# A hybrid encoder block on one core: the memory values computed as a pair of chunks by block products

## The chip, the cores and the metric

The kernel runs on one core of one Trainium2 chip. The metric is the device time of one execution in microseconds (us); lower is better. A core has a matrix engine (TensorE, PE in the profile, with its weight loads as PEld), VectorE (DVE), ScalarE (ACT), GpSimd (POOL) and SyncE (SP), and sixteen DMA engines that SP's, ACT's and POOL's queues feed.

## The reference, cut to what matters

One residual block on x of 256 tokens by 1024 channels, float32: a feed-forward network (SwiGLU, 2816 wide), a mixer (a gated linear recurrence, HGRN2, beside a forgetting attention, FoX, merged by two gates), a cross attention that reads a memory of 256 rows, and a second feed-forward network. Each branch is normalised before and after by a root mean square. The part that is changed most:

```python
def mem_cross_attention(h, mem_n, w_mq, w_mkv, w_mo):
    q = (h @ w_mq).reshape(B, S, MEM_HEADS, MEM_DH)
    k, v = jnp.split(mem_n @ w_mkv, 2, axis=-1)
    ...
    s = jnp.einsum('bqhd,bkhd->bhqk', q, k) * (1.0 / math.sqrt(MEM_DH))
    p = jax.nn.softmax(s, axis=-1)
    o = jnp.einsum('bhqk,bkhd->bqhd', p, v).reshape(B, S, D_MODEL)
    return o @ w_mo

x = x + rmsnorm(mem_cross_attention(rmsnorm(x, mem_pre_g), rmsnorm(mem, mem_kv_g), ...), mem_post_g)
```

## The kernel before, in words

**Numbers as pairs.** Every float32 operand is split into a rounded high part and the rest (`hi` and `lo`, for activations `h` and `l` of a `Pair`), and each product is three matmuls: high by high, high by low, low by high. A weight unit is 128 x 1024 values, 512 KB. `load_split` loads one to a `raw` buffer (four of them), on SP's queue (line 136); ScalarE casts it to `hi` (137) and VectorE makes `lo` by subtraction (138); there are eight buffers each of `hi` and `lo`. `split` does the same for activations (156 and 157). All matmuls are issued on line 93 and recorded in `log`, so the profile has one line for nearly all of them.

**Order.** Each engine runs its own list of instructions in order. The program order is that of the code, but `after(i)` puts what follows it right behind the recorded matmul number i, ahead of what was written before it, and `issue_after` ties one instruction behind another; the constants at the head of the file (`L_...`, `F_T`, `M_O`, `SUMS_AT`) are these places. SP's queue holds the weight loads in order of use, each issued when its buffer comes free.

**Block products.** In pairs of chunks of the feed-forward networks (`quad`), an input of two halves is multiplied with two chunks of weights by seven products of blocks instead of eight: `forms_of`-like sums of the input's blocks are made once (in `mixed`), sums of the weights' blocks are either made on the spot or, for the second network, ahead of time. Three accumulators take part: `b1`, `b2` of the tag `mm` (two buffers) and `b3` of the tag `tr`. `b1` collects the first product, then the second on top of it, then the third, then the fourth; between these, `keep` copies its contents with ScalarE to a `z2` tile.

**Sums made ahead.** A step (`load_step`, `at`) loads two weight units into a `wide` buffer (two of them), adds their blocks by four additions of 128 x 512 on VectorE (lines 771 to 774) and stores them to device memory (776). There are 16 steps, four for each of the four pairs `QUADS_2` of the second feed-forward network, placed by `SUMS_AT` after named projections. The first two steps' loads go on SP's queue, the others' and all stores on POOL's (759, 776). `sum_of` loads the sums back into a `wide` buffer when the pair is computed (450), on SP's queue.

**Stages, in order.** First network; projections `i_a`, `f_a`, `q_a`; the recurrence's chunks interleaved with the projection `gf`; `k_b`, `q_b`, `v_b` of FoX; the four `gates` chunks, with FoX's outputs between them; `br_a` and `br_b`; `w_out`; then the memory block: keys `mk`, queries `mq`, values `mv`, scores, output `mo`; then the second network. The memory, transposed, comes in as `memT` and is multiplied by the gain into the pair `M`; its reciprocal root mean squares `rm` come from a second copy, `ms`. `mk` multiplies each product by the row `rowm` of these and then splits it; `mem_v(c)` (two chunks, 48 matmuls of 128 x 512 each) scales by `rm` when it leaves the accumulator (lines 1236 and 1237). The scores of the two token halves (maxima 1254, exponentials 1258, division 1260, transposes 1264) stand between `mem_v(0)` and `mem_v(1)`; the four `mem_out(i)` multiply probabilities with values, two of them placed inside `mem_v(1)`.

**The end.** `post_last` normalises the last half: sums of squares on ScalarE (243), a square root (357, table of its own), a reciprocal and one Newton step on VectorE (364 to 368), and the last addition into `xs` in three parts, one by ScalarE and POOL with its store on ACT's queue, two on VectorE with stores on SP's. `warm` calls a square root earlier (417), behind the Silu of the last chunk's second half as the code orders it, to load its table.

Of the kernel before, what the change touches and what calls it, by code (L numbers as in the profile page):

```python
# [42 lines left out]
M_O = (24, 36)  # L43
# [16 lines left out]
TO_GATES = 4  # L60
# [18 lines left out]
def block_kernel(ctx: ExitStack, tc: tile.TileContext, wts, head_in, gf_in, x_in, mem_in, memT_in, cols, rows, fbias, masks, out):  # L79
# [44 lines left out]
    loads = []  # L124

# [3 lines left out]
    def load_split(src, n=512):  # L129

        raw = wp.tile([P, D], F32, tag="raw", name=nm("raw"), bufs=4)
        hi, lo = parts_of()
        r, h, l = raw, hi, lo
        if n < 512:
            r, h, l = (p.rearrange("p (k n) -> p k n", k=2)[:, :, :n] for p in (raw, hi, lo))
        loads.append(nc.sync.dma_start(r, src).ins)
        S.copy(h, r)  # L137
        V.tensor_tensor(out=l, in0=r, in1=h.bitcast(F32), op=ALU.subtract)  # L138
        return hi, lo
# [134 lines left out]
    def mixed(X, r, back=0):  # L274

        with after(len(log) - 1 - back):
            row = row_of(r)
        full = [m4([P, 4, T], n="full") for _ in range(2)]
        for f, xh, xl in zip(full, X.h, X.l):
            V.tensor_tensor(out=f, in0=xh.bitcast(F32), in1=xl.bitcast(F32), op=ALU.add)  # L280
            V.tensor_tensor(out=f, in0=f, in1=bc(row, [P, 4, T], 1), op=ALU.mult)
        N = Pair()
        for q in range(2):
            split(N.h[q], N.l[q], full[q])
# [22 lines left out]
        return N, out  # L307
# [38 lines left out]
    def post_last(ps, h, grow, factor):  # L346
# [22 lines left out]
        for eng, a, b, queue in ((G, 512, 768, nc.scalar), (V, 0, 512, nc.sync), (V, 768, 1024, nc.sync)):  # L369
            xh = xs[:, h, a:b]  # L370
            t = ts[a // 512][:, a % 512 : a % 512 + b - a]
            if eng is G:
                S.activation(t, t, AF.Copy, scale=r)
                G.tensor_tensor(out=xh, in0=t, in1=xh, op=ALU.add)
            else:
                V.scalar_tensor_tensor(out=xh, in0=t, scalar=r, in1=xh, op0=ALU.mult, op1=ALU.add)  # L376
            queue.dma_start(out[h * P : (h + 1) * P, a:b], xh)


    def ffn(w_in, w_dn, X, r2, n_tok, i_row, quads, sums, first_half, second_half=None):  # L380
# [28 lines left out]
        def act_evac(ps, c, h):  # L409
# [5 lines left out]
            if c == NFF - 1 and (c, 1 - h) in ats and not first_half:  # L415
# [11 lines left out]
        def quad(c, n_down):  # L427
# [5 lines left out]
            def two(src):  # L433
                hi, lo = (p.rearrange("p (i n) -> p i n", i=2) for p in parts_of())
                split(hi, lo, src)
                return [(hi[:, i], lo[:, i]) for i in range(2)]

            B11, B21 = [], []

            if sums:  # L440
                for i in range(4):
                    hi, lo = load_split(wts[_AT[w_in] + 4 * c + i - 4])
                    B11.append((hi[:, :512], lo[:, :512]))
                    B21.append((hi[:, 512:], lo[:, 512:]))

                def sum_of(k):
                    W = wp.tile([P, 2, D], F32, tag="wide", name=nm("wide"), bufs=2)
                    for q in range(2):
                        with tc.issue_after(loads[-1]):
                            loads.append(nc.sync.dma_start(W[:, q], sums[c][(0, 3, 2, 1)[k], q]).ins)  # L450
                    return two(W[:, 0].rearrange("p (i n) -> p i n", i=2)) + two(W[:, 1].rearrange("p (i n) -> p i n", i=2))

                def lower():
                    out = []
                    for q in range(2):
                        u = _AT[w_in] + 4 * c + 2 * q
                        raw = wp.tile([P, D], F32, tag="raw", name=nm("raw"), bufs=4).rearrange("p (i n) -> p i n", i=2)
                        loads.append(nc.sync.dma_start(raw, wts[u : u + 2, :, 512:].rearrange("i p n -> p i n")).ins)
                        out += two(raw)
                    return out  # L460

                summed = None
            else:
                wide, made = [], [[], [], []]
# [38 lines left out]
            def X(h, j):  # L503
                hs = slice(h * P, h * P + P)
                return lambda i: (N.hi(2 * i + j)[:, hs], N.lo(2 * i + j)[:, hs])

            def F(h, l):
                return lambda i: (h[:, i], l[:, i])

            def prod(ps, A, B, i, start, stop=False):  # L510
                (ah, al), (bh, bl) = A(i), B[i]
                MM(ps, ah, bh, start=start and i == 0, stop=False, skip_group_check=True)
                MM(ps, ah, bl, start=False, stop=False, skip_group_check=True)
                MM(ps, al, bh, start=False, stop=i == 3, skip_group_check=True)

            def prods(ps, A, B, start, stop=False):
                for i in range(4):
                    prod(ps, A, B, i, start, stop)

            def keep(ps):  # L520
                t = sp.tile([P, 512], F32, tag="z2", name=nm("keep"), bufs=3)
                S.copy(t, ps)
                return t

# [609 lines left out]
    for j in range(2):  # L1134
        nc.sync.dma_start(memT_s[j], memT_in[:, 4 * j : 4 * j + 4, :])
# [261 lines left out]
```

## Time and profile before

| | us |
|---|---|
| three runs | 785.2, 785.71, 786.02 |
| the profiled execution | 785.17 |
| its span | 783.4 |
| TensorE busy | 774.3 (99%) |
| VectorE busy | 646.2 (82%) |
| ScalarE busy | 468.4 (60%) |
| GpSimd busy | 48.4 (6%) |
| DMA: mean rate, bytes | 247 GB/s, 193.61 MB |

Busy figures are shares of the span. In rows of groups, the columns are: line, engine, operation, output and inputs with shapes, count, then busy time in all, mean duration of one in ns, and the idle time of the engine just before them with what ended most of it. A timeline row has start, duration, engine, line, operation and count; a chain row has start, length and what ran. In the slices of the span (40 of 19.6 us each) a digit is a busy share in tenths. A row of DMA issues ends with the median time from issue to landing. In the table of windows, each engine's busy time stands in the order PE, PEld, DVE, ACT, POOL, then the granted clock, the DMA share and GB/s.

### The profile page before, as it was taken

The page shows a single profiled execution, that of the slowest core. Times are in us where ns is not written, and L with a number is a line of the kernel's source. Part 1 is how long each engine was busy: PE and PEld are TensorE (multiplying, and loading weights), DVE is VectorE, ACT ScalarE, POOL GpSimd, SP SyncE. Part 2 cuts the span into 40 slices and gives each one's busy share as a digit, 9 for nine tenths or more (in the row PEclk, how much of TensorE's full clock was granted, in tenths as well). Part 3 has the DMA queues.
Part 4 walks back from the last instruction along what each step waited for, and adds up shares of the span by engine and source line. Part 5 has one row for each costly group of instructions (what it writes and reads, how often), then busy time and mean ns, then how long its engine had stood idle before and what let it go on. Part 6 is the DMA issues. An engine that isn't in the chain of part 4 may idle for free.

```text
span 783.4 us, 13175 instructions
## 1 busy us (share of the span) xinstructions
PE 774.3 (99%) x5004; PEld 669.9 (86%) x5004; DVE 646.2 (82%) x1004; ACT 468.4 (60%) x704; POOL 48.4 (6%) x81
## 2 busy tenths in 40 slices
PE   9999999999999999999999999999999999999996
PEld 7888888888899999998888888999888888888884
DVE  7889989968798898578777886998787889888864
ACT  7665664756752447347674444744646758677763
POOL 0000000000121100200001221011110000000000
PEclk9999999999999999999999999999999999999999
DMA  9794484476687655753479999579875279899831
GB/s 349 249 327 154 155 309 161 147 233 245 251 305 257 183 191 164 232 212 121 152 278 341 377 338 378 203 275 375 319 226 185 83 261 388 311 314 323 339 122 54
DMA packets 57392, 193.61 MB, mean 247 GB/s; under 512 B 6249, under 2 KB 9713, under 8 KB 57329
## 3 DMA queue, kind: packets, MB, share of 16 engines
q1 hardware_dynamic: 48080, 159.60, 57.9%
q0 software_dynamic: 9104, 33.04, 12.1%
q8 instruction: 39, 0.64, 0.3%
q14 instruction: 25, 0.20, 0.1%
q10 hardware_dynamic: 144, 0.13, 0.0%
HBM read 174.92 MB, written 17.83 MB: 246 GB/s over the span
## 4 chain that ended last, share of the span: by engine, by line
PE 99%; ACT 0%; DVE 0%; issue 0%; DVEq 0%; ACTq 0%
PE mm L93 64%; PE acc L93 28%; PE tr L93 4%; PE tr L395 1%; PE tr L315 1%; PE tr L1067 0%; PE tr L1158 0%; PE tr L1264 0%; ACT L357 0%; PE tr L406 0%; DVEq L1393 0%; DVE xs L376 0%; ACT hT L156 0%; ACT y L357 0%; ACT junk L243 0%
## 5 line engine op out<-in xcount | busy, mean ns | idle before, releaser
L138 DVE TENSOR_TENSOR lo<-raw,hi 128x1024 fp32r<-128x1024 f32 (+1 forms) x228 | 271.3, 1205 | 53.0 <-ACT hi L137 49.2
L137 ACT CAST hi<-raw 128x1024 fp32r<-128x1024 f32 (+1 forms) x228 | 232.1, 1036 | 118.2 <-PE mm L93 69.5
L93 PE MATMUL mm<-lo,hT 128*128 128x512 f32 (+1 forms) x448 | 171.2, 386 | 0.0
L93 PE MATMUL mm<-hi,hT 128*128 128x512 f32 (+1 forms) x448 | 170.7, 385 | 0.0
L93 PE MATMUL mm<-hi,lT 128*128 128x512 f32 (+1 forms) x448 | 170.4, 384 | 0.0
L93 PE MATMUL acc<-hi,act 128*128 128x512 f32 x352 | 113.2, 391 | 0.0
L93 PE MATMUL mm<-hT,hi 128*128 128x256 f32 x384 | 109.0, 284 | 0.1
L93 PE MATMUL mm<-hT,lo 128*128 128x256 f32 x384 | 109.0, 284 | 0.0
L93 PE MATMUL mm<-lT,hi 128*128 128x256 f32 x384 | 108.9, 284 | 0.0
L93 PEld LDWEIGHTS mm<-hi,hT 128*128 128x128 f32 x448 | 84.1, 188 | 16.1 <-ACT hT L271 0.7
L93 PEld LDWEIGHTS mm<-hi,lT 128*128 128x128 f32 x448 | 84.1, 188 | 15.8 <-DVE lT L272 0.5
L93 PEld LDWEIGHTS mm<-lo,hT 128*128 128x128 f32 x448 | 84.0, 188 | 15.0 <-DVE lo L138 0.4
L93 PEld LDWEIGHTS acc<-hi,act 128*128 128x128 f32 x352 | 65.9, 188 | 13.7 <-DVE act L157 0.2
L93 PEld LDWEIGHTS mm<-hT,hi 128*128 128x128 f32 x384 | 73.6, 192 | 0.5 <-issue 0.3
L93 PEld LDWEIGHTS mm<-lT,hi 128*128 128x128 f32 x384 | 73.6, 192 | 0.1
L93 PEld LDWEIGHTS mm<-hT,lo 128*128 128x128 f32 x384 | 73.6, 192 | 0.1
L93 PE MATMUL acc<-lo,act 128*128 128x512 f32 x176 | 69.0, 392 | 0.0
L157 DVE TENSOR_TENSOR lo<-wide,hi 128x1024 fp32r<-128x1024 f32 x40 | 47.9, 1219 | 1.5 <-ACT hi L156 1.1
L156 ACT CAST hi<-wide 128x1024 fp32r<-128x1024 f32 x40 | 41.5, 1052 | 11.5 <-DVE wide L494 7.5
L776 POOL DMA_DIRECT2D sums<-wide x32 | 23.6, 738 | 357.8 <-DVE wide L773 240.8
L93 PEld LDWEIGHTS acc<-lo,act 128*128 128x128 f32 x176 | 33.1, 188 | 6.7
L93 PE MATMUL mm<-hi,sh 128*128 128x512 f32 x96 | 37.5, 390 | 0.0
(243 smaller groups left out, 1126.8 us busy)
## 6 DMA issues: line engine op xcount, KB each, us to landing
raw<-in_wts_dram SPq DMA_DIRECT2D x232, 512.0 KB, 5.1
sums<-wide POOLq DMA_DIRECT2D x32, 512.0 KB, 6.2
wide<-sums SPq DMA_DIRECT2D x32, 512.0 KB, 6.9
wide<-in_wts_dram POOLq DMA_DIRECT2D x28, 512.0 KB, 6.7
wide<-in_wts_dram SPq DMA_DIRECT2D x12, 512.0 KB, 6.4
raw<-in_gf_dram SPq DMA_DIRECT2D x12, 344.0 KB, 4.9
head<-in_head_dram SPq DMA_DIRECT2D x8, 388.0 KB, 5.7
grow<-in_rows_dram SPq DMA_DIRECT2D x4, 512.0 KB, 8.9
```

The source lines that it names most:

```text
L93: log.append(PE.matmul(*args, **kw).ins)
L137: S.copy(h, r)
L138: V.tensor_tensor(out=l, in0=r, in1=h.bitcast(F32), op=ALU.subtract)
L156: S.copy(hi, src)
L157: V.tensor_tensor(out=lo, in0=src, in1=hi.bitcast(F32), op=ALU.subtract)
L315: PE.transpose(ps[:, j * P : (j + 1) * P], src(kb), ident)
L395: PE.transpose(trv[:, j, h * P : (h + 1) * P], ats[c, h][:, j * P : (j + 1) * P], ident)
L776: G.dma_start(sums[u][2 * e : 2 * e + 2, q, :, i * 512 : i * 512 + 512].rearrange("k p n -> p k n"), W[:, e])
```

## The change

1. The memory values become one pair of chunks in block form. `M` is scaled by `rowm` before it is split (`scale_by`), so `mk` and the values need no scaling of their own; `joined(M)` and `forms_of` make the four sums of `M`'s blocks; `summed_ahead("mv")` loads four weight units, the sums and the lower halves; the scores stand between the products. The helpers of `quad` move out of it unchanged.
2. Four steps of sums more, for this pair, ahead of the others: 20 steps at other places (`SUMS_AT`), the first after `i_a` and six of them among `q_a`, `gf` and FoX's projections, where there were none. A step's loads and stores now all go on SP's queue: the store six weight loads after the additions are written, the next load four later (`later`, `tick`).
3. `brow`, `memT` and `ms` are loaded from POOL's queue instead of SP's; `brow` uses a `z2` tile.
4. Work moves from VectorE to ScalarE: the affine maps of `f` and `k`, `q` by one Silu, `gf` by one Silu, FoX's division by the row sum.
5. `post_last` adds on VectorE alone, in two halves of 512, with both stores on SP's queue; `warm` stands behind the last Silu that is issued.
6. All four `mem_out` stand behind the products; the transposes of probabilities are placed inside them (`L_PT`).

The core of the diff:

```diff
-SUMS_AT = (
-    ("i_a", 1), ("f_a", 0), ("f_a", 2), ("f_a", 3), ("gates", 1), ("gates", 3), ("br_a", 0), ("br_b", 0),
-    ("br_a", 1), ("br_b", 1), ("mk", 1), ("mk", 3), ("mq", 0), ("mq", 1), ("mv", 1), ("ao", 0),
-)
+SUMS_AT = (("i_a", 1), ("f_a", 1), ("f_a", 3), ("q_a",1), ("q_a",3), ("gf",1), ("gf",3), ("gf",5), ("k_b", 1), ("q_b", 1), ("v_b", 3), ("gates", 0), ("gates", 1), ("gates", 2),("gates",3), ("br_a", 0), ("br_b", 0), ("br_a", 1), ("br_b", 1), ("mk", 3),)
+TO_STORE = 6
+TO_LOAD = 4
...
+    def later(n, f):
+        due.append((len(loads) + n, f))
+
+    def tick():
+        while due and due[0][0] <= len(loads):
+            due.pop(0)[1]()
...
+    def joined(X):
+        full = [m4([P, 4, T], n="full") for _ in range(2)]
+        for f, xh, xl in zip(full, X.h, X.l):
+            V.tensor_tensor(out=f, in0=xh.bitcast(F32), in1=xl.bitcast(F32), op=ALU.add)
+        return full
...
+    def scale_by(full, row):
+        for f in full:
+            V.tensor_tensor(out=f, in0=f, in1=bc(row, [P, 4, T], 1), op=ALU.mult)
...
-        for eng, a, b, queue in ((G, 512, 768, nc.scalar), (V, 0, 512, nc.sync), (V, 768, 1024, nc.sync)):
...
+        for j, (t, xh) in enumerate(zip(ts, x_halves(h))):
+            V.scalar_tensor_tensor(out=xh, in0=t, scalar=r, in1=xh, op0=ALU.mult, op1=ALU.add)
+            nc.sync.dma_start(out[h * P : (h + 1) * P, j * 512 : (j + 1) * 512], xh)
...
-            if c == NFF - 1 and (c, 1 - h) in ats and not first_half:
+            if len(ats) == 2 * NFF - 1 and not first_half:
                 with tc.issue_after(silu.ins):
                     S.activation(warm, ones[:, 0:1], AF.Sqrt)
...
+    pairs = [("mv", 0)] + [("f2_in", c) for c in QUADS_2]
...
-                if len(slots) < 2:
-                    with tc.issue_after(loads[-1]):
-                        nc.sync.dma_start(part, src)
-                else:
-                    G.dma_start(part, src)
+            with tc.issue_after(loads[-1]):
+                nc.sync.dma_start(W[:, e].rearrange("p j n -> p (j n)"), wts[_AT[name] + 4 * (c + e - 1) + 2 * q + i])
...
-        for e in range(2):
-            G.dma_start(sums[u][2 * e : 2 * e + 2, q, :, i * 512 : i * 512 + 512].rearrange("k p n -> p k n"), W[:, e])
-        load_step()
+        def store():
+            for e in range(2):
+                with tc.issue_after(loads[-1]):
+                    nc.sync.dma_start(sums[u][2 * e : 2 * e + 2, q, :, i * 512 : i * 512 + 512].rearrange("k p n -> p k n"), W[:, e])
+            later(TO_LOAD, load_step)
+        later(TO_STORE, store)
...
-                V.tensor_scalar(out=f[:, i], in0=f[:, i], scalar1=olb[:, hd : hd + 1], scalar2=lbv[:, hd : hd + 1], op0=ALU.mult, op1=ALU.add)
+                S.activation(f[:, i], f[:, i], AF.Identity, bias=lbv[:, hd : hd + 1], scale=olb[:, hd : hd + 1])
...
-            V.tensor_tensor(out=z, in0=ps, in1=bc(row2, [P, 2, T], 1), op=ALU.mult)
-            S.activation(q[:, js], z, AF.Sigmoid)
-            V.tensor_tensor(out=q[:, js], in0=q[:, js], in1=z, op=ALU.mult)
+            V.tensor_tensor(out=q[:, js], in0=ps, in1=bc(row2, [P, 2, T], 1), op=ALU.mult)
+            with tc.issue_after(k_last):
+                S.activation(q[:, js], q[:, js], AF.Silu)
+            at("q_a", 2 * c + j)
...
-            sig_last = S.activation(sg, ps[:, :n], AF.Sigmoid, scale=r2[h]).ins
-            V.scalar_tensor_tensor(out=Gt[h][:, c * GF : c * GF + n], in0=ps[:, :n], scalar=r2[h], in1=sg, op0=ALU.mult, op1=ALU.mult)
+            sig_last = S.activation(Gt[h][:, c * GF : c * GF + n], ps[:, :n], AF.Silu, scale=r2[h]).ins
...
-            nc.sync.dma_start(brow, rows[4 + c // 2, c % 2 * 512 : c % 2 * 512 + 512].partition_broadcast(P))
+        G.dma_start(brow, rows[4 + c // 2, c % 2 * 512 : c % 2 * 512 + 512].partition_broadcast(P))
...
+    gates(1)
+    with after(len(log) - L_RM):
+        rowm = row_of(rm)
+    scale_by(memT_s, rowm)
+    M = Pair()
+    for c in range(2, 4):
+        gates(c)
+        for kb in range(4 * c - 8, 4 * c - 4):
+            gain_split(M, kb, memT_s[kb // 4][:, kb % 4, :], G_KV)
...
-    rowm = row_of(rm)
+    for kb in range(4, 8):
+        unit("w_out", kb)
+    (s1h, s1l), (s2h, s2l), (s3h, s3l), (s4h, s4l) = forms_of(joined(M))
...
-    def mem_v(c):
...
+    B11, B21, sum_of, lower = summed_ahead(_AT["mv"], sums["mv", 0])
+    b1, b2, b3 = mm(), mm(), trp()
+    for i in range(4):
+        prod(b1, block(M, 0, 0), B11, i, True)
+        prod(b3, block(M, 0, 1), B21, i, True, True)
+    scores(0)
+    p1 = keep(b1)
+    prods(b2, form_of(s1h, s1l), sum_of(0), True)
+    V.tensor_tensor(out=p1, in0=p1, in1=b3, op=ALU.add)
+    values(0, 0, p1)
+    T2 = sum_of(1)
+    T3 = sum_of(2)
+    scores(1)
+    prods(b1, form_of(s2h, s2l), T2, False)
+    w = keep(b1)
+    m = len(log)
+    prods(b1, form_of(s3h, s3l), T3, False)
+    with after(m + L_PT[0]):
+        probs_T(0)
+    v = keep(b1)
+    V.tensor_tensor(out=v, in0=b2, in1=v, op=ALU.subtract)
+    values(1, 1, v)
+    prods(b1, block(M, 1, 1), sum_of(3), False, True)
+    values(0, 1, b1)
+    with after(m + L_PT[1]):
+        probs_T(1)
+    prods(b2, form_of(s4h, s4l), lower(), False, True)
+    V.tensor_tensor(out=w, in0=b2, in1=w, op=ALU.subtract)
+    values(1, 0, w)
```

More of the change, by code (lines that the diff above doesn't have):

```diff
@@ L42 @@
 L_Y = 16
[L43 removed]
+L_RM = 1
+L_PT = (6, 23)
 R_AT = (18, 52, 86, 120, 160, 206, 252, 298, 344)
@@ L280, in mixed, with forms_of @@
             V.tensor_tensor(out=f, in0=xh.bitcast(F32), in1=xl.bitcast(F32), op=ALU.add)
[L281 to L284, printed above, removed]
+        return full
+    def forms_of(full):
         sums = [m4([P, 2, 4, P], n="sums") for _ in range(2)]
@@ L1282, in mem_out @@
         split(AO.h[i // 2][:, i2], AO.l[i // 2][:, i2], ps.rearrange("p (a t) -> p a t", a=2))
[L1284 to L1290 removed]
+    for i in range(4):
         mem_out(i)
[L1292 removed]
     X4 = Pair()
```

207 lines of the change are left out of this document (97 added, 110 removed).

## The prediction, on record before the run

> **What bounds the kernel now.** I read the page first, then TensorE's waits, then the chain of waits around the memory block, then the groups by form there, the timeline of the end, and the table by windows of the stretch into which new work goes. The page, with engine shares, tenths by slice and the chain:
>
> ```profile
> span 783.4 us, 13175 instructions
> PE 774.3 (99%) x5004; PEld 669.9 (86%) x5004; DVE 646.2 (82%) x1004; ACT 468.4 (60%) x704; POOL 48.4 (6%) x81
> ...
> DVE  7889989968798898578777886998787889888864
> ...
> DMA  9794484476687655753479999579875279899831
> ...
> PE 99%; ACT 0%; DVE 0%; issue 0%; DVEq 0%; ACTq 0%
> ...
> L137 ACT CAST hi<-raw 128x1024 fp32r<-128x1024 f32 (+1 forms) x228 | 232.1, 1036 | 118.2 <-PE mm L93 69.5
> ```
>
> TensorE's waits, all of them in one row:
>
> ```profile
> PE tr L93 <- DVE ones L206: 1.1, 1, 1.1
> ```
>
> TensorE is busy 99% of the span, 99% of the chain that ended last is TensorE, and its one wait is 1.1 us at the start. So there is hardly a wait left that an edit could remove: before the last matmul, only fewer matmuls can win time, and any new wait of TensorE is paid in full. The cast row says that ScalarE mostly waits for TensorE to release a buffer: as a rule the split weights are ahead of their use.
>
> The profiled execution took 785.17 us, of which 783.4 are the span and 1.77 lie around it. It is 0.54 below the median of the three runs, 785.71. The sum below is made against 785.17; the forecast of a median adds the 0.54 back. A difference of 0.2%, 1.57 us, is about what a measurement of this kernel can tell from none.
>
> **Prices.** The chain of waits between 520 and 640 us (start, us, what, count):
>
> ```profile
> 551.86 5.75 PE acc L93 x48
> ...
> 561.73 0.87 PE tr L1264 x8
> ...
> 572.65 0.59 ACT hT L156
> ...
> 577.81 18.65 PE acc L93 x82
> ```
>
> The last row is 128x512 matmuls back to back: 18.65/82 = 0.227 us each. The first is 128x256: 5.75/48 = 0.120. Eight transposes take 0.87. A group's mean for a 128x512 matmul is longer than that (0.39), since matmuls overlap; the difference of 0.16 is what passes between the last issue and its end. Groups by form, 540 to 600 us, first VectorE, then ScalarE (count, busy, mean ns, idle before):
>
> ```profile
> L138 DVE TENSOR_TENSOR lo<-raw,hi 128x1024 fp32r<-128x1024 f32 x19 | 22.9, 1218 | 4.1 <-ACT hi L137 4.0
> L157 DVE TENSOR_TENSOR lT<-tr,hT 128x512 fp32r<-128x512 f32 x8 | 5.2, 685 | 3.7 <-ACT hT L156 3.7
> L1254 DVE TENSOR_REDUCE mx<-acc 128x1 f32<-128x256 f32 x8 | 3.0, 414 | 0.6 <-PE acc L93 0.6
> L1260 DVE TENSOR_TENSOR pm<-pm,sm 128x1024 f32<-128x1024 f32 x2 | 2.5, 1225 | 0.1
> L773 DVE TENSOR_TENSOR wide<-wide 128x512 f32<-128x512 f32 x3 | 2.1, 689 | 0.1
> ```
> ```profile
> L137 ACT CAST hi<-raw 128x1024 fp32r<-128x1024 f32 x18 | 18.8, 1055 | 7.0 <-PE acc L93 5.4 <-DMA raw<-in_wts_dram 0.8 <-PE mm L93 0.7
> L1258 ACT ACTIVATE pm<-acc,mx,sc 128x256 f32<-128x256 f32 x8 | 4.4, 570 | 1.6 <-DVE mx L1255 1.6
> L156 ACT CAST hT<-tr 128x512 fp32r<-128x512 f32 x8 | 4.4, 588 | 8.1 <-PE tr L93 4.6 <-PE tr L1264 3.5
> ```
>
> Neighbours overlap by about 0.08: the timelines there show two `lo` in 2.35 us and two casts in 2.02. I therefore count 1.14 for a 128x1024 `lo` or `pm`, 0.97 for a cast, 0.61 for a 128x512 VectorE pass, 0.72 for a pair of maxima, 0.55 for an exponential, 0.5 for an `hT` evacuation, 0.58 for a `keep` copy (as that cast, with nothing before it).
>
> ```profile
> 553.58 0.74 DVE L1254 TENSOR_REDUCE mx<-acc 128x1 f32<-128x256 f32 x2
> ...
> 569.85 2.35 DVE L138 TENSOR_TENSOR lo<-raw,hi 128x1024 fp32r<-128x1024 f32 x2
> ```
> ```profile
> 565.91 2.02 ACT L137 CAST hi<-raw 128x1024 fp32r<-128x1024 f32 x2
> ```
>
> **Part 1, the memory values.** Removed: `mem_v` has 8 units x 12 = 96 matmuls of 128x512; the block form has 7 products x 12 = 84. 12 x 0.227 = **-2.72 us**, all on the path.
>
> **Part 2, waits that the block form adds.** Before, each product had its own accumulator and nobody waited. Now `b1` is added to in four products, and its contents are copied between them (`keep`), so TensorE must wait for two copies, w and v. Put zero at the first product's first matmul. TensorE's own time: 24 matmuls 5.45; `scores(0)`, 24 x 0.120, to 8.33; T1 to 11.05; `scores(1)` to 13.93; T2 to 16.65. Then it waits for `w`: 0.16 until the last matmul ends, a weight cast queued ahead on ScalarE until 17.15, 0.58 of copy: third product from about 17.75 instead of 16.65, **+1.1**. Seven matmuls to 19.34, eight transposes of `pm` of the first half, five matmuls, then `v` must be copied.
>
> What these stand behind is VectorE's order. The third sum's load needs a `wide` buffer (there are two), which T1's second `lo` releases some 1.1 us after zero (two casts and two `lo` around the end of `mq`). From its landing L, VectorE runs without a gap to `pm`: cast 0.97, then six `lo` 6.84, four pairs of maxima 2.9, `keep` addition and `lT` 1.22, small ones 0.3, `pm` 1.2: 13.4 in all. Behind `pm`, ScalarE must do three exponentials of the second half (their maxima are scaled after `pm`), an `hT`, the fourth exponential, an `hT`, and only then the copy of `v`: 0.15 + 1.65 + 0.5 + 0.55 + 0.5 + 0.58, about 4.0. How long do loads of such sums take? The DMA view, with medians, and the minimum, median and maximum of that issue line:
>
> ```profile
> raw<-in_wts_dram SPq DMA_DIRECT2D x232, 512.0 KB, 5.1
> sums<-wide POOLq DMA_DIRECT2D x32, 512.0 KB, 6.2
> wide<-sums SPq DMA_DIRECT2D x32, 512.0 KB, 6.9
> wide<-in_wts_dram POOLq DMA_DIRECT2D x28, 512.0 KB, 6.7
> ```
> ```profile
> DMA to landing us min/median/max: 3.4/6.9/9.1
> ```
>
> Those 32 stand in the second FFN, where the DMA tenths are mostly 8 and 9; here eight loads are out before zero and only four follow soon, so I take 4.3, near the fast end. L = 1.1 + 4.3 = 5.4, `pm` at 18.8 (in time for 19.34), `v` copied at 22.9, while TensorE reaches that point at 19.34 + 0.87 + 1.14 = 21.35: **+1.5**. Sum of Part 2: **+2.6**. Lower end: two bare copies, 2 x (0.16 + 0.58), 1.5. Upper end, landing after the median 6.9: `pm` at 21.4 (+2.1), `v` at 25.5 against 23.4 (+2.1), with `w` 5.3. Behind it (fourth and lower product, `mem_out`) I find VectorE in time by 0.3 to 1 us, so nothing more.
>
> The Trainium skill ("PSUM — Partial Sum Buffer", Engine vs sequencer instructions) says that matmuls start and complete in program order, which speaks against this change: nothing placed behind the waiting product can fill its gap. The trace has the same in small, at 572.65, where the chain passes over 0.59 of `hT`. A TensorE that could pass on would lose nothing here, and the sum would be 2.6 lower.
>
> **Part 3, the end.** The timeline of the last 8 us:
>
> ```profile
> 775.78 0.60 ACT L243 ACTIVATE junk<-acc 128x512 f32<-128x512 f32 x1 [2.03 <-PE acc L93]
> 776.27 0.19 ACT L243 ACTIVATION_READ_ACCUMULATOR junk<-acc 128x1 f32 x1
> 776.49 1.28 ACT L357 ACT_TABLE_LOAD   x1
> 776.50 0.69 DVE L361 SCALAR_TENSOR_TENSOR post<-acc,grow 128x512 f32<-128x512 f32 x1 [1.24 <-ACT junk L243]
> 777.11 0.15 DVE L359 TENSOR_TENSOR v<-ss,v 128x1 f32<-128x1 f32 x1
> 777.78 0.29 ACT L357 ACTIVATE y<-ss,v 128x1 f32<-128x1 f32 x1
> 778.11 0.17 DVE L364 RECIPROCAL y<-y 128x1 f32<-128x1 f32 x1 [0.85 <-ACT y L357]
> ...
> 778.76 1.61 DVE L376 SCALAR_TENSOR_TENSOR xs<-post,y,xs 128x512 f32<-128x512 f32 x2
> 779.35 0.73 POOL L374 TENSOR_TENSOR xs<-post,xs 128x256 f32<-128x256 f32 x1 [193.38 <-ACT post L373]
> 779.54 1.19 SPq L377 DMA_DIRECT2D out_dram<-xs  x2
> ```
>
> The root's table is loaded at 776.49, on the path, because the earlier `warm` load was undone by a later Silu. `warm` now stands after the last Silu, so the root runs at 776.5 and the reciprocal follows `v`, at 777.28 instead of 778.11: 0.83 earlier. Two 128x512 passes in place of 512 and 256 take about 1.4 instead of 1.61 (the 256 was slow beside POOL's addition); the last store, of 256 KB instead of 128, lands a little later. I take **-0.9** (ends -0.6 and -1.1).
>
> The Trainium skill ("ScalarE: Activation LUTs", What ACT_TABLE_LOAD costs) gives 1283 ns for a load and some 1380 ns of drain with it; by that the end would win 1.4 us more. This trace agrees on the 1.28 and shows no drain: the accumulator's read ends at 776.46, the load starts at 776.49 and the root 0.01 after it. So the rule's drain gets no share of the chances.
>
> **Part 4, the rest, on engines that TensorE does not wait for today.** Four steps more of sums (16 additions of 0.61, 9.8 us of VectorE), three of them in the `gf` stretch; against them `f`, `k`, `q`, `gf` and FoX's division go to ScalarE. The table of windows there, and the row of the `gf` multiply that goes:
>
> ```profile
> 260.00:270.00 10.00, 10.00 (x221) 9.69 (x211) 9.78 (x15) 4.07 (x6) 1.04 (x3) 1.00 0.67 193
> 270.00:280.00 10.00, 10.00 (x223) 9.54 (x224) 8.57 (x16) 5.40 (x7) 1.23 (x4) 1.00 0.55 186
> 280.00:290.00 10.00, 9.95 (x288) 9.41 (x277) 9.97 (x19) 5.84 (x7) 0.00 (x0) 1.00 0.60 190
> 290.00:300.00 10.00, 10.00 (x202) 9.80 (x202) 9.20 (x22) 4.57 (x8) 0.51 (x1) 1.00 0.38 132
> ```
> ```profile
> L947 DVE SCALAR_TENSOR_TENSOR G<-mm,rstd,z 128x344 f32<-128x344 f32 x4 | 2.3, 565 | 0.6 <-ACT z L946 0.6
> ```
>
> VectorE (the third busy figure) is filled 37.5 of 40 us. Three steps add 12 x 0.61 = 7.3, six multiplies take 3.4 away: 41.4, or 1.4 too much. Before TensorE feels it, the lead of the split weights must be used up. Steps now share SP's queue with the weights: a step's load stands behind its predecessor's store, with one to four weight loads between; in the tightest place (the end of `gf`) VectorE has 14.6 us of its own work between the step that is stored and the addition that needs the load (four `lo` of 688 columns at 0.8, two of 1024, four additions, eight passes of 512, 1.8 of small ones), against 6.2 + 6.7 for store and load, so SP's order should just not stop VectorE. `brow`, `memT` and `ms` go to POOL, one behind the other; `rowm` needs them in time for transposes in `gates`. Bounds: 0 if all stays covered, +2.5 if both this chain and the 1.4 come through. I take **+0.5**, near the covered end, because the cast row shows a lead and TensorE's wait row nothing.
>
> **Sum.** -2.72 + 2.6 - 0.9 + 0.5 = -0.5: 784.7 on the profiled execution, **785.2** as a median.
>
> **The rivals.**
> 1. *The products cover the waits.* If the third sum lands in 3.4 and ScalarE is free for the copies, Part 2 is 1.5 and Part 4 is 0: -2.72 + 1.5 - 0.9 = -2.1, median 783.6. For it: queues are quiet here, and VectorE idles 4 us on 60 behind casts. Against: exponentials stand ahead of `v`.
> 2. *The third sum lands late* (this ends slower). At the median 6.9 the whole chain `pm`, exponentials, `v` slides: -2.72 + 5.3 - 0.9 + 0.5 = +2.2, median 787.9. It decides the sign from a landing of about 5.4 (each us of landing costs up to two). For it: the median itself. Against: the quiet queue.
> 3. *VectorE becomes the bound in the `gf` stretch*, where it is at 37.5 of 40: the 1.4, plus a step's load waited for in its strict order, some 1 to 2 us: median 787.5 to 788. For it: the tenths. Against: the lead.
>
> That the change removes fewer matmuls than it says is no case: the counts stand in the loops.
>
> **How the numbers follow.** Forecast, between 784.1 and 787.3: 0.37. Rival 1: 0.29; rival 2: 0.18; rival 3: 0.16. Faster by over 0.2% is rival 1, slower by over 0.2% rivals 2 and 3 (0.34), the rest is the forecast's. The range reaches from Part 2 at its lower end with the end at -1.1 and something hidden besides (782.9) to Part 2 at 5.3 and Part 4 at 2.5 (790.1, cut to 789.5 as both are rarely met together).
>
> **What would show it.** TensorE's waits list ScalarE's `keep` copies, with about 1.1 and 1.5 us, and nothing over 0.5 us between 180 and 320 us; the last table load stands before 770 us, and the reciprocal starts 1.5 us after the last `junk` instead of 2.3. Transposes waiting for `pm` say rival 2, TensorE waiting for `lo` or `q` around 260 to 320 rival 3. If TensorE's waits sum to less than 1.5, Part 2 was wrong.

## The result and the profile after

The changed kernel takes **804.82 us** (median of 6 runs, 801.14 to 810.25) against 785.19 before (median of 6, 784.9 to 786.02): a ratio of **1.0253, 95% interval 1.023 to 1.0276**. It is slower by 19.6 us, and its runs spread eight times as wide. The forecast was 785.2 with a range to 789.5. The profiled execution took 801.14, the fastest of the six, with a span of 799.4; what follows is read from it, so it explains 16 of the 19.6 us.

The page of the changed kernel: span, engines, and the chain that ended last by engine.

```profile
span 799.4 us, 13175 instructions
PE 778.1 (97%) x4992; PEld 670.0 (84%) x4992; DVE 653.0 (82%) x1015; ACT 487.7 (61%) x739; POOL 12.6 (2%) x28
...
PE 78%; DMA 9%; DVE 7%; ACT 4%; issue 2%; SPq 0%; DVEq 0%; ACTq 0%
```

TensorE runs the 12 instructions fewer that were promised (4992 for 5004). But it is idle for 799.4 - 778.1 = 21.3 us where it was idle for 9.1, and it is *busy* 3.8 us longer in spite of fewer matmuls. The 16.0 us of the span are these two: 12.2 of idling and 3.8 of slower work. And the chain, which was TensorE to 99%, now goes through DMA, VectorE and ScalarE for a fifth of the span.

TensorE's two longest waits (us in total, times, longest), then what ScalarE's casts wait for, after and, in the third fence, before:

```profile
PE mm L92 <- ACT keep L351: 4.1, 2, 3.0
PE tr L92 <- DVE ct L1053: 3.9, 1, 3.9
```
```profile
ACT hi L144 <- DMA raw<-in_wts_dram: 89.2, 75, 5.8
```
```profile
ACT hi L137 <- PE mm L93: 69.5, 52, 7.6
ACT hi L137 <- DMA raw<-in_wts_dram: 25.3, 33, 2.7
```

Before, a cast mostly waited for TensorE to give a buffer back: weights lay ready. Now casts wait 89 us in all for the weights themselves. The lead on which the prediction's Part 4 rested is gone. Where it goes, the windows show (busy times of PE, PEld, DVE, ACT, POOL, then clock, DMA share, GB/s), first before (with a later stretch at a high rate), then after:

```profile
240.00:260.00 20.00, 20.00 (x260) 19.78 (x262) 15.54 (x25) 8.34 (x12) 2.02 (x4) 1.00 0.65 204
260.00:280.00 20.00, 20.00 (x442) 19.23 (x434) 18.35 (x30) 9.47 (x13) 2.27 (x6) 1.00 0.61 189
280.00:300.00 20.00, 19.95 (x488) 19.21 (x477) 19.16 (x40) 10.41 (x15) 0.51 (x1) 1.00 0.49 161
300.00:320.00 20.00, 20.00 (x244) 19.62 (x244) 15.24 (x22) 12.64 (x22) 2.08 (x4) 1.00 0.67 198
320.00:340.00 20.00, 20.00 (x170) 20.00 (x169) 10.18 (x13) 7.24 (x8) 3.57 (x4) 1.00 0.73 254
...
420.00:440.00 20.00, 20.00 (x90) 16.56 (x89) 15.81 (x18) 9.40 (x9) 2.69 (x5) 1.00 1.01 388
440.00:460.00 20.00, 20.00 (x93) 16.45 (x92) 17.06 (x22) 9.32 (x10) 5.14 (x8) 1.00 0.98 350
460.00:480.00 20.00, 20.00 (x93) 16.48 (x93) 16.73 (x22) 7.41 (x9) 5.11 (x8) 1.00 0.94 355
```
```profile
240.00:260.00 20.00, 20.00 (x228) 19.78 (x226) 14.85 (x24) 9.51 (x13) 0.00 (x0) 1.00 0.92 317
260.00:280.00 20.00, 18.06 (x406) 17.04 (x393) 17.27 (x27) 7.33 (x11) 2.26 (x6) 0.91 1.00 348
280.00:300.00 20.00, 19.50 (x480) 18.59 (x481) 19.82 (x41) 9.93 (x12) 0.00 (x0) 1.00 0.89 312
300.00:320.00 20.00, 20.00 (x274) 19.54 (x267) 20.00 (x35) 11.64 (x22) 1.59 (x2) 1.00 0.87 296
320.00:340.00 20.00, 19.90 (x168) 19.70 (x167) 10.42 (x15) 7.27 (x8) 3.74 (x5) 1.00 0.98 352
340.00:360.00 20.00, 16.10 (x113) 14.80 (x112) 15.81 (x40) 11.04 (x20) 0.00 (x0) 0.91 0.74 261
```

From 240 to 340 us the DMA engines moved 201 GB/s on average, at a share of 0.63; now it is 325, at 0.93: 12.4 MB more in 100 us (124 GB/s x 100 us). These bytes are the steps'. Eight of the 20 stand among `q_a` (two), `gf` (three) and FoX's projections (three); "six" in the list of changes is too few. They issue 16 loads and 16 stores of 512 KB from 240 to 340 us, where the kernel before issued two and two. A weight load there takes 6.4 us (median) from issue to landing; before, it took 4.5.

TensorE idles 6.4 us between 240 and 360 us (0.1 before), most of it at 350. Another 4.1 us of idling lie between 560 and 600 us, in the memory block (0.1 before).

A high DMA share alone does not do this. From 420 to 480 us the kernel before ran at shares of 0.94 to 1.01, and TensorE idled nowhere; weight loads landed in 6.4 us (median, 420 to 500 us) there too. One difference is VectorE. It was busy 15.8 to 17.1 of 20 us there; in the changed kernel it is busy 19.8 and 20.0 of 20 us from 280 to 320 us.

The chain of waits into the wait for `ct` shows the loss being made:

```profile
300.20 4.67 DMA raw<-in_wts_dram
...
315.38 6.33 DMA raw<-in_wts_dram
...
328.24 8.51 DMA raw<-in_wts_dram
...
339.18 6.46 DMA raw<-in_wts_dram
...
349.87 3.74 DMA raw<-in_wts_dram
...
354.54 0.10 DVE ct L1053
```

Five landings of weights take 29.7 of the 54.3 us. Between them stand casts and VectorE's work in its order, additions of steps among it. SP's queue stands still too: between 240 and 360 us, steps' stores wait there 28.1 us for additions and steps' loads 26.3 us for stores to land, with weight loads behind them.

The "slower work" is in good part the clock. The same columns in windows of 1 us around the wait for `ct`:

```profile
355.00:356.00 1.00, 1.00 (x9) 0.97 (x8) 1.00 (x6) 0.09 (x1) 0.00 (x0) 0.85 0.65 193
356.00:357.00 1.00, 1.00 (x4) 0.74 (x3) 1.00 (x2) 0.00 (x0) 0.00 (x0) 0.50 0.81 299
357.00:358.00 1.00, 1.00 (x4) 0.81 (x3) 1.00 (x7) 0.00 (x0) 0.00 (x0) 0.50 0.30 123
358.00:359.00 1.00, 1.00 (x3) 0.78 (x3) 1.00 (x4) 0.04 (x1) 0.00 (x0) 0.50 0.00 0
359.00:360.00 1.00, 1.00 (x6) 0.85 (x5) 0.71 (x5) 1.00 (x5) 0.00 (x0) 0.94 0.00 0
```

TensorE stands still for 3.9 us, starts again at 354.7, and within a microsecond its granted clock falls to 0.50 for three more: 0.15 + 3 x 0.5 + 0.06 = 1.7 us lost on top of the 3.9. It happens twice in this execution (the other place is at the end of this document): 3.4 us of the 6.5 by which TensorE's work is slower (3.8 more, and 2.7 that the matmuls left out should have saved). The other three I cannot place.

### The profile page after: what moved, and what is told of

Same layout as the page of the kernel before. It is cut to its first block, busy times and chain, and to the rows that moved or that the text cites. A ratio compares the mean times of both kernels' runs of the same rounds, so it can differ in the third digit from the quotient of the medians.

```text
span 799.4 us, 13175 instructions
## 1 busy us (share of the span) xinstructions
PE 778.1 (97%) x4992; PEld 670.0 (84%) x4992; DVE 653.0 (82%) x1015; ACT 487.7 (61%) x739; POOL 12.6 (2%) x28
## 4 chain that ended last, share of the span: by engine, by line
PE 78%; DMA 9%; DVE 7%; ACT 4%; issue 2%; SPq 0%; DVEq 0%; ACTq 0%
PE mm L92 47%; PE acc L92 25%; DMA raw<-in_wts_dram 6%; PE tr L92 3%; DVE lo L145 2%; ACT hi L144 2%; DMA raw<-in_gf_dram 1%; DMA sums_f_in<-wide 1%; PE tr L464 1%; PE tr L390 1%; DVE wide L794 0%; DVE q L928 0%; DVE lo L165 0%; DMA head<-in_head_dram 0%; DVE wide L793 0%
## 5 line engine op out<-in xcount | busy, mean ns | idle before, releaser
L145 DVE TENSOR_TENSOR lo<-raw,hi 128x1024 fp32r<-128x1024 f32 (+1 forms) x224 | 266.1, 1202 | 71.5 <-ACT hi L144 69.2
L144 ACT CAST hi<-raw 128x1024 fp32r<-128x1024 f32 (+1 forms) x224 | 230.0, 1036 | 140.8 <-DMA raw<-in_wts_dram 89.2
L92 PE MATMUL mm<-hi,hT 128*128 128x512 f32 (+1 forms) x424 | 162.7, 388 | 1.2 <-ACT keep L351 1.1
L92 PE MATMUL mm<-lo,hT 128*128 128x512 f32 (+1 forms) x424 | 163.3, 389 | 0.4 <-DVE lo L145 0.4
L92 PE MATMUL mm<-hi,lT 128*128 128x512 f32 (+1 forms) x424 | 162.7, 388 | 0.0
L92 PEld LDWEIGHTS mm<-lo,hT 128*128 128x128 f32 x424 | 80.3, 190 | 15.2 <-DVE lo L145 1.3
L92 PEld LDWEIGHTS mm<-hi,lT 128*128 128x128 f32 x424 | 80.3, 190 | 15.0 <-DVE lT L280 0.5
L165 DVE TENSOR_TENSOR lo<-wide,hi 128x1024 fp32r<-128x1024 f32 x48 | 57.7, 1221 | 9.6 <-ACT hi L164 9.1
L164 ACT CAST hi<-wide 128x1024 fp32r<-128x1024 f32 x48 | 49.5, 1050 | 20.6 <-DVE wide L537 7.5
L92 PE MATMUL mm<-hi,sh 128*128 128x512 f32 x112 | 44.0, 393 | 3.0 <-ACT keep L351 3.0
L92 PE MATMUL mm<-lo,sh 128*128 128x512 f32 x112 | 43.8, 391 | 0.0
L92 PE MATMUL mm<-hi,sl 128*128 128x512 f32 x112 | 43.7, 390 | 0.0
```

Source lines behind the costliest of these rows:

```text
L92: log.append(PE.matmul(*args, **kw).ins)
L164: S.copy(hi, src)
L165: V.tensor_tensor(out=lo, in0=src, in1=hi.bitcast(F32), op=ALU.subtract)
```

## The experiments

Two groups of theories. For the projections and the recurrence: **Q**, weights stand behind waiting instructions in SP's queue; **V**, VectorE is full; **A**, ScalarE's new work delays the casts; **B**, too many bytes. For the memory block: whether its waits eat what its products save. All ratios are against runs of the kernel before on the same chip.

**The end alone, on the kernel before** (`e4_tail_only`):

```diff
-        for eng, a, b, queue in ((G, 512, 768, nc.scalar), (V, 0, 512, nc.sync), (V, 768, 1024, nc.sync)):
...
+        for j, (t, xh) in enumerate(zip(ts, x_halves(h))):
...
-            if c == NFF - 1 and (c, 1 - h) in ats and not first_half:
+            if len(ats) == 2 * NFF - 1 and not first_half:
```

> The kernel before with the changed end alone: the last addition on VectorE in two halves with both stores on SP's queue, and the square root's table loaded behind the last Silu. The reading of the profile before gives -0.9 (784.3), the last table load before 770 us and the reciprocal 1.5 us after the last sum of squares starts instead of 2.3. If the store or POOL set the end instead, no change (785.2).

784.37, ratio 0.9989 (0.998 to 0.9998): -0.9 as forecast, and the one version here that beats both kernels, if narrowly: the interval allows 0.2 to 1.6 us. Its timeline:

```profile
776.78 0.60 ACT L243 ACTIVATE junk<-acc 128x512 f32<-128x512 f32 x1 [2.03 <-PE acc L93]
...
777.50 0.29 ACT L357 ACTIVATE y<-ss,v 128x1 f32<-128x1 f32 x1
...
778.18 0.16 DVE L364 RECIPROCAL y<-y 128x1 f32<-128x1 f32 x1
```

The root follows the last sum of squares with no table load between them, and the reciprocal starts 1.40 after `junk` (2.33 before).

**The steps' transfers back on POOL's queue** (`e1_steps_pool`), and the gates' loads back on SP's as well (`e2_pool_gates_sp`):

```diff
-                    nc.sync.dma_start(sums[u][...], W[:, e])
+            G.dma_start(sums[u][...], W[:, e])
...
-        G.dma_start(brow, ...)
+            nc.sync.dma_start(brow, ...)
```

> The changed kernel with one part undone: the loads and stores of the sum steps go back to POOL's queue (each store right behind its additions, the next load right behind the store); places of the steps, additions and all else stay. Theory Q (SP's queue): weight loads stand behind step stores that wait for VectorE and behind step loads that wait for a store to land, so weights come late and VectorE, which takes them in order, and then TensorE wait. Q expects 790 to 795, the waits between 250 and 360 us gone, and ScalarE's casts waiting for weights some 25 us in all instead of 89. Theory V (VectorE is full where four more steps were put): 801 or more, as the additions stay where they are.

> As the run before, and the loads of brow, memT and ms go back to SP's queue as well, so that all queues are those of the kernel before. Q expects 788 to 793, with TensorE's waits for the reciprocal row of the memory (about 1.5 us around 422 us in the changed kernel) gone too; if POOL's steps had delayed brow and memT in the run before, this one is the faster by more than 2 us. V expects 801 or more.

807.43 (1.0284, 1.0266 to 1.0301) and 808.36 (1.0302, 1.0265 to 1.0339): no better than the change. Q's figures missed by more than ten, so the choice of the queue is not the cause; V's 801 or more is met by both. In `e1_steps_pool` SP's queue no longer waits for steps between 240 and 360 us, but the loss takes another way. On POOL's queue a step's load now stands right behind the store before it, and the chain of waits holds a store of 10.2 us (from 276.7) and the next load of 7.1 (to 295.0) before VectorE can add. The Trainium skill ("DMA: Bandwidth & Descriptors", Issuing engines are not separate DMA queues) says that issuing from several engines saves only the sequencer's time; these two runs, in which no time was saved, agree.

**Without the additions** (`e3_no_adds`): the four additions of each step are left out.

> The changed kernel without the additions of the sum steps (80 VectorE instructions of 0.61 us, 49 us in all, left out, so the sums that are stored are the plain weight blocks); all loads and stores of the steps stay on SP's queue. V expects VectorE relieved and 787 to 791. Q expects that most of the loss stays, 797 to 803, since stores and loads still stand in SP's queue ahead of weights; the stores then wait for the loads to land instead of for VectorE.

802.28 (1.0216, 1.0194 to 1.0238). 49 us of VectorE are gone and 2.5 us come back: V alone is not the cause either. The time lies in Q's range, but Q's waits are mostly gone as well: between 240 and 360 us steps in SP's queue wait 5.5 us, all for stores to land, instead of 54.4 (28.1 + 26.3). TensorE still idles 5.0 us there. So the loss needs neither, though its pieces shift: the longest wait is now 5.2 us for the reciprocals made from `ms`.

**ScalarE's new work back on VectorE** (`e8_no_act_moves`):

```diff
-                S.activation(f[:, i], f[:, i], AF.Identity, bias=..., scale=...)
+                V.tensor_scalar(out=f[:, i], in0=f[:, i], scalar1=..., scalar2=..., op0=ALU.mult, op1=ALU.add)
```

> The changed kernel with the work that went from VectorE to ScalarE put back (maps of f and k, q's and gf's Silu as a sigmoid and a product, FoX's division). A expects 800 or less. B expects no gain, 803 to 809, as no byte changes; more than 807 would say that VectorE is short there.

814.72 (1.0373, 1.0317 to 1.0428), 10 us slower than the change. A falls. The expectation took more than 807 as a sign that VectorE is short, and so it is: in the changed kernel VectorE's time counts. The same moves on the kernel before, with the changed end (`e15_tail_and_moves`):

> The kernel before with the changed end and the moves from VectorE to ScalarE (f, k, q, gf, FoX's division), nothing else: no more bytes, the same steps at the same places and queues. The moves take VectorE off work while TensorE does not wait, so 784.4 as with the end alone. 786 or more would say that ScalarE's new work delays casts; under 784 that VectorE held TensorE up somewhere.

785.2 (1.0006, 0.9997 to 1.0014). There the moves gain nothing; rather, the 0.9 of the end is gone, so that they may cost some 0.8 us. The two intervals just touch.

**A quarter of the bytes** (`e7_quarter`): as many transfers at the same places; QP is 32.

```diff
-                nc.sync.dma_start(W[:, e]..., wts[...])
+                nc.sync.dma_start(W[:QP, e]..., wts[..., :QP])
...
-                    nc.sync.dma_start(sums[u][2 * e : 2 * e + 2, q, :, ...], W[:, e])
+                    nc.sync.dma_start(sums[u][2 * e : 2 * e + 2, q, :QP, ...], W[:QP, e])
```

> The changed kernel with the same number of step loads and stores at the same places in SP's queue and with the same waits, but each moves 32 of 128 rows, a quarter of the bytes (the additions too are on 32 rows, which does not shorten them; the block products read plain weights in place of the sums). B expects 787 to 792. If order and waits in SP's queue cost the time, most stays: 798 or more.

**787.67** (1.0032, 1.0017 to 1.0048): 17 of 19.6 us are back, and the spread is down to 785.67 to 790.15. The windows of that run:

```profile
260.00:280.00 20.00, 20.00 (x486) 19.34 (x485) 19.85 (x33) 8.08 (x11) 2.27 (x6) 1.00 0.75 224
...
340.00:360.00 20.00, 20.00 (x124) 17.81 (x122) 19.01 (x59) 12.88 (x38) 0.00 (x0) 1.00 0.36 124
```

VectorE is busier than in the changed kernel (19.85 for 17.27 from 260 to 280 us), and TensorE does not wait in these windows; weight loads land in 4.3 us again (median, 240 to 340 us). B stands. One thing comes with the bytes: small stores land sooner. Between 240 and 360 us steps' loads wait 2.2 us for them in SP's queue instead of 26.3, while the stores' waits for additions grow from 28.1 to 37.1. So this run alone does not part the bytes from waits for stores; the run without additions above and the one with bytes alone below do.

Small stores alone, with full loads (`e10_small_stores`):

> The changed kernel with full loads of the steps and stores of a quarter (32 of 128 rows; the block products read plain weights). Theory B counts bytes, whoever writes them: half of the 17 us that a quarter of all bytes gave back, 793 to 798. If the stores alone cost the time (a load of the next step waits for a store to land), 790 or less; if the loads alone, 801 or more.

793.51 (1.0105, 1.0091 to 1.0119): 11 of the 17 us. Bytes count in both directions, the stores somewhat more. TensorE's wait for `ct` stays, at 3.8 us.

**Bytes alone, on the kernel before** (`e13_before_more_bytes`): five times four copies between q_a and the end of gf; no work needs what they move.

```diff
+    def more_bytes():
+        for _ in range(4):
+            n = len(copies)
+            copies.append(1)
+            with tc.issue_after(loads[-1]):
+                loads.append(nc.sync.dma_start(spare[n], wts[n]).ins)
```

> The kernel before with nothing but bytes added: 20 copies of 512 KB of weights from device memory to an unused part of it, four at each of five places from q_a to the end of gf, issued on SP's queue without a wait for anything (so that only their issue, some 0.4 us each, and their bytes stand ahead of weight loads). B expects 788 to 797, with ScalarE's casts waiting for weights. If waits of SP's queue for stores and for VectorE were needed for the loss, 787 or less.

**800.49** (1.0191, 1.0166 to 1.0217), more than the 788 to 797 that B expected. Bytes suffice: SP's queue waits 1.1 us for the copies, and for no addition that the kernel before did not have. The windows, TensorE's longest wait, and the chain of waits that leads to it and on:

```profile
240.00:260.00 20.00, 14.31 (x106) 14.14 (x105) 10.72 (x16) 4.02 (x6) 2.02 (x4) 0.83 0.86 312
260.00:280.00 20.00, 17.91 (x352) 17.31 (x351) 16.00 (x25) 8.20 (x12) 0.00 (x0) 0.91 1.02 370
```
```profile
PE mm L93 <- DVE z L843: 5.7, 1, 5.7
```
```profile
236.05 10.22 DMA wide<-in_wts_dram
...
246.39 0.69 DVE wide L781
...
259.98 8.12 DMA raw<-in_gf_dram
```

The 5.7 us are not a wait for weights. VectorE, in its order, stands before the additions of a step that the kernel before has at this place too; the step's load took 10.2 us (that kernel's median is 6.7), and `z` stands behind the additions. Weights come late further on (8.1 us). So added bytes delay whatever VectorE must take in order, a step's load as well as a weight.

Two limits of this run: its copies read and write device memory at once, so that memory sees up to twice the traffic of as many step transfers; and they stand ahead of weights in SP's queue, which is not tested apart.

**Other places.** Three steps moved out of gf (`e6_gf_free`), and 16 steps with none between q_a and q_b (`e5_sixteen`):

> The changed kernel with the three steps in the gf stretch moved to v_b and mk; 20 steps, all on SP's queue as in the change. B expects part of the loss back, 793 to 799: no late weights around 260 to 290 us, those behind k_b and q_b less late. If the order in SP's queue costs the time and not the bytes, 801 or more, since as many steps stand in it.

> The changed kernel with 16 steps of sums instead of 20, none between q_a and q_b, on POOL's queue; the block products of the memory values are all done, but read the sums of the second network's first pair (so the values themselves are not those of the reference). Theory B (bytes): the changed kernel asks the DMA engines for more than they move between 240 and 340 us, in whatever queue, and weights land late from there on. B expects 786 to 790: what is left over the kernel before is the memory block's waits. Theory A (ScalarE's new work delays the casts of weights) expects 798 or more, as that work is untouched.

799.35 (1.02, 1.0172 to 1.0228): 5.5 back, just short of the 793 to 799 that B expected. From 280 to 360 us nothing is lost any more, but TensorE waits 4.7 us for `keep`. The second gave 801.53 (1.0215, 1.0199 to 1.0231) where 786 to 790 was expected: a miss. Its trace has no loss from 240 to 480 us. It comes later: 3.4 us at `xs` in w_out, and in the memory block 4.6 and 4.1 for `hi` and `lo` of split operands. The steps at mq now store there. Two of SP's waits for the sums' buffers, between 540 and 590 us:

```profile
SPq L373 <- DMA sums_f_in<-wide: 10.0, 2, 8.8
SPq L373 <- DMA wide<-sums_f_in: 8.8, 2, 6.0
```

So without steps in the first stretch nothing is lost there. That the two `wide` buffers, which the stores hold, cause the loss in the memory block is read from these waits; no run tests it.

**The block products.** Undone, on the quarter bytes (`e9_quarter_mem_v`), and with the second scores moved behind the second product (`e12_quarter_covered`, whose edit this is):

```diff
-    scores(1)
     prods(b1, form_of(s2h, s2l), T2, False)
     w = keep(b1)
+    scores(1)
```

> The run with quarter bytes again (same parts left out), with the block products undone as well: the values are made by 96 matmuls as before, from the scaled M, with the scores between the two chunks; the sums of M's blocks go. In the run with quarter bytes TensorE lost 2.8 us around the block products and 1.6 at w_out, where VectorE makes the sums, against 2.72 us of matmuls saved. If these waits are the price of the block form, this one is the same or faster by up to 2 us, 785.5 to 788. If they have another cause it is slower by up to 2.7, 788.5 to 790.5.

> The run with quarter bytes again, with the scores of the second half moved from ahead of the second product to behind it, so that 24 matmuls (2.88 us) stand between that product and the third, which waits for the copy of w. By Part 2 of the prediction the wait for w goes (about 1 us) but the exponentials ahead of the copy of v come later, so that one grows by up to 2: 787 to 790. If the copies are the whole price, 786 to 787.

788.01 (1.0034, 1.0021 to 1.0048) without the block products, 787.67 with them: no difference that their spread could show. Of the 2.72 us that 84 matmuls save over 96, the waits for `keep` alone take 2.0. The reordered one took 789.9 (1.0065, 1.0052 to 1.0078): its wait for `w` is 0.6 us instead of 1.4, that for `v` 3.4 instead of 0.7, as Part 2's chain says (exponentials later, the copy behind them later).

**What is left at a quarter of the bytes** (3.6 us over the kernel before with the changed end): without the additions (`e14_quarter_mem_v_no_adds`), and with the gates' loads on SP's queue (`e16_quarter_mem_v_gates_sp`).

> The run with quarter bytes and the block products undone (788.0), now also without the 80 additions of the sum steps. It has the changed end, worth 0.9, and still stood 3.6 above the kernel before with that end. If the additions on VectorE are what is left (rival 3 of the prediction: 1.4 us and more), 785 to 786. If the moves to ScalarE, the queues of the gates' loads or the scaling of M are, 787 or more.

> The run with quarter bytes and the block products undone (788.0), with brow, memT and ms loaded from SP's queue as in the kernel before. If POOL's queue makes the memory's reciprocals late (TensorE waits 0.4 us for them there), 787 to 787.6; otherwise 788 or more, as SP's queue is the fuller one.

Both missed, upwards: 794.9 (1.0146, 1.0131 to 1.0162) and 796.79 (1.0154, 1.014 to 1.0168). In the first, the memory's copy `ms` lands 11.9 us after its issue instead of 10.6, and TensorE waits for the reciprocals made from it:

```profile
PE tr L93 <- DVE y L234: 3.6, 1, 3.6
```
In the second, the chain of waits shows, twice between 440 and 490 us, a loop that needs few bytes:

```profile
470.22 0.31 SPq L800
...
473.00 6.67 DMA wide<-in_wts_dram
479.69 0.67 DVE wide L792
480.36 1.15 DVE lo L146
```

SP's store waits for VectorE's last addition; the next load stands behind the store; VectorE, in its order, waits for that load before it may make the `lo` that TensorE needs. The waits of theory Q are therefore not needed for the 17 us, but they are a second way to lose, here after nothing but three kinds of loads changed queues. Which edits make up the 3.6 us stays open. I can place 2.5 of them in TensorE's waits in `e9_quarter_mem_v`: 1.3 for `zf` behind the additions in gf, 0.8 for `xs` at w_out and 0.4 for the reciprocals. The moves to ScalarE may have a part in the rest, 0.8 by `e15_tail_and_moves`.

## Why the prediction was wrong

**Bounds: right.** TensorE had no slack, and each new wait was paid in full. It was paid more than in full: the price of a wait left out the clock after it.

**Part 1: right.** 12 instructions fewer; their 2.72 us are not to be seen in the total, as TensorE's remaining work was slower.

**Part 2: right in mechanism, too small in one term.** TensorE waits for the two copies, 4.1 us instead of 2.6 and inside the upper end of 5.3. The landing was the term: I took 4.3 us for the sums, and the eight loads of the memory's sums measure (minimum, median, maximum):

```profile
DMA to landing us min/median/max: 6.0/6.7/7.6
```

That is close to the median of 6.9 which I had refused for a quiet queue (rival 2). It hit the copy of `w` (3.0 us) more than that of `v` (1.1), the other way round from the forecast. ScalarE first waits 5.4 us for a sum and then works without a gap until `w` is copied. Ahead of that copy stand a table load and four exponentials that I had put into no sum for `w`. ScalarE's timeline:

```profile
563.57 1.05 ACT L164 CAST hi<-wide 128x1024 fp32r<-128x1024 f32 x1 [5.44 <-DMA wide<-sums_mv]
...
570.07 1.28 ACT L1281 ACT_TABLE_LOAD   x1
...
574.05 1.06 ACT L144 CAST hi<-raw 128x1024 fp32r<-128x1024 f32 x1
575.00 0.60 ACT L351 COPY keep<-mm 128x512 f32<-128x512 f32 x1
```

**Part 3: right.** -0.9, measured alone (0.2 to 1.6).

**Part 4: the step that failed.** It was taken at +0.5 with an upper end of +2.5. Leaving out three quarters of the steps' bytes gives 17 us back, about 2 of them at `keep`. The step is the one that settled the figure: "near the covered end, because the cast row shows a lead". That lead was the kernel's before, and the new transfers used it up: casts wait 89.2 us for weights instead of 25.3, and weights from 240 to 340 us land in 6.4 us instead of 4.5. The prediction asked of each new transfer whether it *waits* too long, and never what it does to the weights beside it: eight steps of four times 512 KB, 2.1 MB each, into a stretch whose windows it quoted for VectorE's column only, with the DMA share in the same rows. It also counted VectorE from 260 to 300 us alone. There it was not overfilled (37.1 of 40 us busy), but with the steps among FoX's projections it went from 15.2 to 20.0 of 20 us from 300 to 320, ahead of the longest wait.

One piece of Part 4 held: "SP's order should just not stop VectorE". The steps' loads and stores from 240 to 340 us landed in 5.2 and 5.7 us (medians), under the 6.7 and 6.2 that it used, and the list of VectorE's waits in the changed kernel has none for a step's load. Nor would the rate by itself have settled the matter: 325 GB/s are less than the 350 to 388 at which the kernel before lost nothing from 420 to 480 us. Why the stretch from 240 us on is the more sensitive one is not shown. A nearly full VectorE is one candidate: work put back on it cost 10 us more, but the additions taken off it gave only 2.5 back.

**The rivals.** Rival 3 had the place and the sign, with a chance of 0.16 and 1 to 2 us. Its first cause, VectorE overfilled, is refuted as the sole one by the run without additions; its second, VectorE waiting in its order for a step's load, is not met in the changed kernel, but in `e1_steps_pool` and `e13_before_more_bytes`. Rival 2 was right on the landing, which is a small part of the loss. Rival 1 is refuted.

## What to carry to other kernels

Before adding work that only moves data, sum the bytes of each stretch, and ask what later landings do to the loads that already stand there: a lead read from the kernel before need not outlast the change. A rate below the best window of the same kernel is no proof of slack; 325 GB/s did harm in one stretch where 350 to 388 had done none in another. Test it by cutting the bytes and keeping every instruction, and beside it by adding bytes alone to the kernel before: small transfers also land sooner, so the first run shortens waits together with bytes. And a reordered product that saves matmuls on an engine without slack is worth only what its accumulator's copies leave of it.

## What the runs showed of the hardware

A stall of TensorE can be followed by a stretch at half clock: 0.50 from about 355.8 to 359.1 us after 3.9 us of standing. A shorter stall did it too, behind 113 matmuls of 128x16 that together took 1.16 us. The chain of the changed kernel has 1.65 us without work there, and the windows behind it, as above, show the clock:

```profile
268.13 1.65 issue
```
```profile
271.00:272.00 1.00, 1.00 (x5) 1.00 (x5) 1.00 (x4) 0.00 (x0) 0.89 (x3) 0.50 0.83 272
272.00:273.00 1.00, 1.00 (x5) 1.00 (x4) 1.00 (x3) 0.00 (x0) 0.85 (x3) 0.50 0.90 350
```

Yet the 3.0 us for `keep` at 572.7 were followed by none:

```profile
576.00:577.00 1.00, 1.00 (x6) 0.82 (x5) 1.00 (x3) 0.64 (x2) 0.00 (x0) 1.00 0.72 242
```

The Trainium skill ("TensorE: Matmul & The Clock Gate", Part 1: The HAM clock gate) says that an idle window of about 3.4 us halves the clock until as long a busy one has passed. The length at half clock agrees, and so do the 3.9 us, which were followed by it, and the 3.0, which were not; the 1.65 us do not. Whether the small matmuls ahead of them count as idling, no run here tests.
